# Projections of a hybrid attention layer on 16-bit parts instead of 32-bit parts

## The chip, the cores and the metric

The kernel runs on one core of a Trainium2 chip. A core has a matrix engine (TensorE, in the profile PE, with its weight loads as PEld), three engines for elementwise work (VectorE = DVE, ScalarE = ACT, GpSimd = POOL), a queue that issues transfers (SyncE = SP) and 16 DMA engines. Each engine works through its own instructions in the order in which they stand; semaphores make one engine wait for another. The metric is the device time of one launch in microseconds, lower is better.

## The reference

One layer over a sequence of 1024 positions with width 1024. The input is normalised and modulated, then one input projection gives everything that 16 heads of 64 need; 8 heads are softmax attention with a forget gate, 8 are stick-breaking attention; each head's output is gated, and one output projection and a second normalisation follow.

```python
u = _layer_norm(x) * (1.0 + scale) + shift            # scale, shift, gate from silu(c) @ w_ada + b_ada
h = u @ w_in                                           # q, k, v, gate of each group, 8 forget logits
fox: s = q k^T / 8 + F_q - F_k ; causal ; softmax ; p v
sb:  z = q k^T / 8 ; w_ij = sigmoid(z_ij) * prod of sigmoid(-z_im) for j < m < i ; w v
y = concat(y_fox * silu(fg), y_sb * silu(sg)) @ w_out
out = _layer_norm(ALPHA * x + gate * y, ln_g, ln_b)    # all float32
```

## The kernel before, in words

**Precision.** Each large product is made of three matmuls on two parts of each operand: a first part of fewer bits and the rest. In the input projections both parts are of type f32r (`u_hi`, `u_lo` and, for the weights, `whi`, `wlo`; the profile's 32-bit matmuls, written f32). In the products of the attention weights with v, from pair 2 on, both sides are in 16-bit floats (f16).

**Work.** The heads are taken in 8 pairs. Pairs 0 to 3 are stick-breaking heads, 4 to 7 forget-gate heads. A pair has 16 units (head, row block of 128 queries): unit 0 to 15 of pair 0 are here called units 0 to 15, the next are 16 and on. Pair 0 takes row blocks 0 to 3 of both heads first, so that units 8 to 11 are row blocks 4 to 7 of its first head and 12 to 15 those of its second. A stick-breaking unit goes through these steps: scores `S` on PE (L611, L613); two sigmoids on ACT into `kp` (L646) and `be` (L648); a running product over `kp` on DVE (L654, L658); the product `be * kp` on POOL (L660). In pairs 0 and 1 PE then turns `be` (L691, tile `T`), ACT and DVE take it out of PSUM in two parts (L693, L694), and PE multiplies with v (L720). Two units lie between a unit's scores and its turn: the scores of unit k + 2 stand on PE behind the turn of unit k.

**Projections as filler.** The projection of pair 0 (and parts of pair 1) is made in a start phase. The others are generators that are cut into steps; a step of a q, k or gate projection is three matmuls of 512 columns (`m_step`, L329 to L331), a step of a v projection six of 256 or 264 (`v_tile`, L441 to L443). A table of numbers (`FILL`, by pair) sets how many steps stand between the units on PE. In `order` of names: tile `m_p_x_c` is the projection of pair p, x = 0 for q, 1 for k, 2 for gate, of half c of the sequence.

**Preparing weights.** `fetch_w` (L140 to L146) loads 512 columns of a weight matrix (256 KB), and POOL makes the two parts: a copy with rounding (L144) and a subtraction (L145). This happens for 50 pieces in the filler phase. For v of groups 1 to 3 a bound is needed, too, since what v meets there is in f16: `gen_ranges` loads those 12 pieces a second time and DVE sums their squares (L396), all in pair 0.

**What sets the order.** PE's order is the order of the program. On ACT, DVE and POOL a scheduler puts the instructions into an order before the run; on the chip this order is fixed.

**End.** The last gate projection (`gen_last_g`) runs in the first units of pair 7; between its steps the output weights are put in two parts (L1071 on ACT, L1072 on DVE and POOL), into the room of `u_hi` and `u_lo`. Then the output projection follows (L1112 to L1114).

## Time and profile before

Three runs: 665.35, 664.29 and 663.5 us, median 664.29 us. The profiled execution took 664.71 us; its span in the profile is 663.0 us, so 1.7 us lie around it. Times below are microseconds from the span's start.

| part | from, to | span | PE | DVE | ACT | POOL |
|---|---|---|---|---|---|---|
| start phase | 0 to 79.6 | 79.6 | 77.5 | 62.1 | 47.8 | 31.0 |
| pair 0 | 79.6 to 148.8 | 69.2 | 61.7 | 58.3 | 42.3 | 47.9 |
| pair 1 | 148.8 to 221.6 | 72.8 | 72.8 | 54.0 | 44.7 | 41.1 |
| pair 2 | 221.6 to 285.9 | 64.3 | 61.8 | 56.1 | 47.9 | 47.4 |
| pair 3 | 285.9 to 346.1 | 60.2 | 60.2 | 49.8 | 44.4 | 42.6 |
| pairs 4 to 6 | 346.1 to 523.6 | 177.5 | 177.1 | 133.0 | 123.8 | 65.9 |
| pair 7 | 523.6 to 585.0 | 61.4 | 54.1 | 46.8 | 41.4 | 38.0 |
| end | 585.0 to 663.0 | 78.0 | 70.4 | 51.7 | 5.5 | 30.4 |

The columns are busy time. A matmul counts as busy from its start to its modelled end, and the next one starts well before that end, so what a matmul costs in a row of matmuls is read from the distance between starts. POOL's columns and those of the other elementwise engines can be added up.

### The profile page before, as it was taken

To read this page: it belongs to the slowest core of one execution; us is meant where nothing else is said; L and a number is where in the kernel's file an instruction comes from. 1 tells how busy PE (TensorE), PEld (TensorE's weight loads), DVE (VectorE), ACT (ScalarE), POOL (GpSimd) and SP (SyncE) were. 2 spreads that over 40 slices of the span, in tenths; PEclk is the share of its full clock that TensorE was granted. 3 is DMA by queue.
4 is the path that set the end of the run, shared out by engine and by line. 5 is a ranking of instruction groups with operands and counts; after the bars stand their busy time and mean duration, and the time that the engine had idled before them with its cause. 6 is when DMAs were issued, how large, how long until landed. Compare 5 with 4: busy or idle time off the path is not lost. (4 is left out here: it accounts for less than half of the span.)

```text
span 663.0 us, 10902 instructions
## 1 busy us (share of the span) xinstructions
PE 635.6 (96%) x3558; PEld 535.5 (81%) x3558; DVE 511.8 (77%) x1011; ACT 397.8 (60%) x833; POOL 344.3 (52%) x429
## 2 busy tenths in 40 slices
PE   8999989799999999999999999999999979999995
PEld 5789878688899877788998888889888857788884
DVE  6787889886867797978877685867678875986656
ACT  5577347575656867767867675767668886530000
POOL 5660177666645677778666333330643266475412
PEclk9999989899999999999999999999999989999998
DMA  9983543321210255858476666666496997983201
GB/s 319 402 312 135 167 123 110 104 58 28 58 33 10 71 115 112 160 118 157 106 172 153 174 139 153 139 147 125 115 198 137 245 284 176 205 232 129 94 33 63
DMA packets 153800, 96.25 MB, mean 145 GB/s; under 512 B 118224, under 2 KB 133136, under 8 KB 153744
## 3 DMA queue, kind: packets, MB, share of 16 engines
q1 hardware_dynamic: 152160, 91.09, 54.1%
q10 hardware_dynamic: 1584, 4.47, 2.2%
q8 instruction: 28, 0.46, 0.3%
q14 instruction: 28, 0.23, 0.1%
HBM read 55.13 MB, written 7.90 MB: 95 GB/s over the span
## 5 line engine op out<-in xcount | busy, mean ns | idle before, releaser
L329 PE MATMUL m<-uh,whi 128*128 128x512 f32 x304 | 123.0, 405 | 1.2 <-DVE kl L316 1.2
L331 PE MATMUL m<-uh,wlo 128*128 128x512 f32 x304 | 119.8, 394 | 0.0
L330 PE MATMUL m<-ul,whi 128*128 128x512 f32 x304 | 119.8, 394 | 0.0
L660 POOL TENSOR_TENSOR be<-be,kp 128x127 f32<-128x127 f32 (+3 forms) x64 | 89.9, 1405 | 44.9 <-DVE kp L658 24.2
L741 POOL TENSOR_TENSOR ty<-ty,sg 64x256 f32<-64x256 f32 x64 | 49.8, 779 | 91.6 <-DVE ty L736 56.0
L654 DVE TENSOR_TENSOR_SCAN kp<-kp,floor 128x128 f32<-128x128 f32 (+3 forms) x64 | 58.5, 914 | 14.8 <-ACT kp L646 14.1
L611 PE MATMUL S<-k,q 128*128 128x512 f32 (+4 forms) x192 | 68.5, 358 | 1.0 <-ACT be L648 1.0
L331 PEld LDWEIGHTS m<-uh,wlo 128*128 128x128 f32 x304 | 57.2, 188 | 13.6
L329 PEld LDWEIGHTS m<-uh,whi 128*128 128x128 f32 x304 | 57.4, 189 | 12.0 <-PE m L331 1.2
L613 PE MATMUL S<-kl,qz 128*128 128x512 f32 (+4 forms) x192 | 65.8, 344 | 0.0
L330 PEld LDWEIGHTS m<-ul,whi 128*128 128x128 f32 x304 | 57.4, 189 | 9.7
L622 DVE CUSTOM_DVE_ANT_0 a<-S,fb 128x1024 f32<-128x1024 f32 (+7 forms) x64 | 48.2, 753 | 19.7 <-PE S L613 15.8
L628 ACT ACTIVATE a<-a,nm 128x1024 f32<-128x1024 f32 (+7 forms) x64 | 49.7, 776 | 19.8 <-DVE nm L622 18.9
L638 DVE SCALAR_TENSOR_TENSOR home<-a,l,home 128x1024 f16<-128x1024 f32 (+7 forms) x64 | 58.1, 907 | 3.5 <-ACT home L634 3.3
L634 ACT ACTIVATE home<-a,l 128x1024 f16<-128x1024 f32 (+7 forms) x64 | 49.3, 773 | 16.2 <-DVE l L630 9.0
L646 ACT ACTIVATE kp<-S 128x384 f32<-128x384 f32 (+4 forms) x96 | 43.7, 491 | 23.7 <-PE S L613 21.9
L709 PE MATMUL pv<-home,v_g 128*128 128x256 f16 x480 | 56.3, 265 | 0.7 <-DVE ty L736 0.7
L709 PEld LDWEIGHTS <-v_g 128*128 128x128 f16 x480 | 44.2, 99 | 15.1 <-issue 9.8
L441 PE MATMUL v<-whi_v,uh 128*128 128x256 f32 (+1 forms) x192 | 54.7, 285 | 0.0
L443 PE MATMUL v<-wlo_v,uh 128*128 128x256 f32 (+1 forms) x192 | 54.4, 283 | 0.0
L442 PE MATMUL v<-whi_v,ul 128*128 128x256 f32 (+1 forms) x192 | 54.1, 282 | 0.0
L1112 PE MATMUL o<-woh,whi_y 128*128 128x512 f32 (+1 forms) x119 | 47.4, 398 | 5.4 <-DVE sg L322 4.8
(327 smaller groups left out, 1614.3 us busy)
## 6 DMA issues: line engine op xcount, KB each, us to landing
raw<-in_w_qkg_dram SPq DMA_DIRECT2D x38, 256.0 KB, 2.8
wss<-in_w_ss_dram SPq DMA_DIRECT2D x14, 512.0 KB, 8.4
x<-in_x_dram SPq DMA_DIRECT2D x8, 512.0 KB, 6.9
...
```

The source lines that it names most:

```text
L329: nc.tensor.matmul(acc, hi[:, c], u_hi[kt][:, s], start=(kt == 0), stop=False)
L330: nc.tensor.matmul(acc, hi[:, c], u_lo[kt][:, s], start=False, stop=False)
L331: nc.tensor.matmul(acc, lo[:, c], u_hi[kt][:, s], start=False, stop=(kt == NB - 1))
L441: nc.tensor.matmul(acc[:, :n], u_hi[kt][:, ts_], hi[:, s], start=(kt == 0), stop=False)
L442: nc.tensor.matmul(acc[:, :n], u_lo[kt][:, ts_], hi[:, s], start=False, stop=False)
L443: nc.tensor.matmul(acc[:, :n], u_hi[kt][:, ts_], lo[:, s], start=False, stop=(kt == NB - 1))
L611: nc.tensor.matmul(S[:, s, :w], qst[p][h][:, qs], kst[p][h][:, ks], start=True, stop=False)
L613: nc.tensor.matmul(S[:, s, :w], z, klo[p][:, ks], start=False, stop=not masked)
L638: lows[:] = [nc.vector.scalar_tensor_tensor(lo, ab, l, hi, op0=ALU.mult, op1=ALU.subtract)]
L654: last_dve = nc.vector.tensor_tensor_scan(rv, rv, floor[:, :ke - lo], initial=0.0, op0=ALU.mult, op1=ALU.max)
L660: nc.gpsimd.tensor_tensor(be[:, :ke - 1], be[:, :ke - 1], kp[:, 1:ke], op=ALU.mult)
L709: nc.tensor.matmul(acc[:, q0:256], vt[p][:, kb, h * P:(h + 1) * P], pt[:, 2 * kb + x_, q0:], start=(kb == 0 and x_ == 0), stop=(kb == last ...
```

## The change

From the gate projection of pair 1 on, u and the weights are used as two f16 parts each, still with three matmuls per product. To keep f16 in range, u is scaled with a bound (the largest |scale| + |shift|), and each weight matrix with its norm. The norms of one to three matrices ("a batch", 13 in all) are made together: ACT squares and sums the raw pieces (`square`), PE sums over partitions, DVE and POOL make the factors (`scales`); the inverse factors are folded into the instructions that take the results out of PSUM. u is converted once, in 16 pieces of 128 x 512 (`u_convert`): POOL adds `u_hi` and `u_lo` into one room `u_sum`, ACT makes the first part, DVE the rest; the results take the room of `u_hi`. One room serves all 16 pieces, so POOL's next sum waits until ACT and DVE have read the one before. `split16` puts a weight piece in parts: for pairs up to 3 ACT makes the first part, and POOL scales and subtracts; for later pairs POOL does all three. `gen_ranges` and its second loads are gone. Pair 1's gate and pair 2's q and k are taken half by half, with tiles of v between them, and the steps in which nothing was done are taken out of `FILL`. The output weights take other rooms.

```diff
+    C0 = (4, 3.2)
+    C1 = (34, 3.4)
+    BATCHES = (
+        ((14, 1), 22, 26, (((1, 2), (28, 29)), ((2, 0), (33, 37)))),
+        ((30, 1), 35, 38, (((2, 1), (41, 44)),)),
+        ((36, 2), 46, 50, (((1, 3), (52, 54, 56, 58)),)),
...
     def m_step(acc, tiles, kt, ch):
-        hi, lo = tiles[kt // 4]
+        two = tiles[kt // 4]
         c = slice((kt % 4) * P, (kt % 4) * P + P)
-        s = slice(ch * 512, ch * 512 + 512)
-        nc.tensor.matmul(acc, hi[:, c], u_hi[kt][:, s], start=(kt == 0), stop=False)
-        nc.tensor.matmul(acc, hi[:, c], u_lo[kt][:, s], start=False, stop=False)
-        nc.tensor.matmul(acc, lo[:, c], u_hi[kt][:, s], start=False, stop=(kt == NB - 1))
+        nc.tensor.matmul(acc, two[:, 0, c], u_part(kt, 0, ch), start=(kt == 0), stop=False)
+        nc.tensor.matmul(acc, two[:, 0, c], u_part(kt, 1, ch), start=False, stop=False)
+        nc.tensor.matmul(acc, two[:, 1, c], u_part(kt, 0, ch), start=False, stop=(kt == NB - 1))
...
+    def u_convert(kb, ch):
+        if not u_rooms:
+            u_rooms.append(raw_tile("u_sum"))
...
+        full = u_rooms[0]
+        nc.gpsimd.tensor_tensor(full, u_hi[kb][ch].bitcast(F32), u_lo[kb][ch].bitcast(F32), op=ALU.add)
+        nc.scalar.activation(two[:, 0, :], full, AF.Copy, scale=u_up)
+        nc.vector.scalar_tensor_tensor(two[:, 1, :], full, u_up, two[:, 0, :], op0=ALU.mult, op1=ALU.subtract)
...
-        for g in range(1, 4):
-            n = 528 if g == 1 else 512
-            for h in range(4):
-                raw = raw_tile(f"n{g}_{h}")[:, :n]
-                nc.sync.dma_start(raw, w_vf[h] if g == 1 else w_v[g - 1, h])
-                at = 4 * g - 4 + h
-                nc.vector.tensor_tensor_reduce(out=raw, in0=raw, in1=raw, op0=ALU.mult, op1=ALU.add, scale=1.0,
-                                               scalar=0.0, accum_out=fr[:, at:at + 1])
...
+    def square(batch):
+        at = 6 * (n_batch[0] % 2)
+        for i, key in enumerate(k for pm in batch for k in halves_of(*pm)):
+            raw = raw16[key]
+            nc.scalar.activation(rooms[1].bitcast(BF16)[:, :raw.shape[1]], raw, AF.Square,
+                                 accum_out=sums[:, at + i:at + i + 1])
...
+    def scales(batch, ps_n):
...
+        nc.vector.tensor_copy(sums16, sums[:, at:at + n])
+        nc.tensor.matmul(ps_n[:, :n], ones16.to_broadcast([P, P]), sums16, start=True, stop=True)
...
+            nc.vector.tensor_reduce(out=n2[:, x_:x_ + 1], in_=ps_n[:, col:col + k], op=ALU.add,
+                                    axis=mybir.AxisListType.X)
...
+        nc.gpsimd.tensor_tensor(up, n2[:, :k], mhalf.to_broadcast([P, k]), op=ALU.pow)
+        nc.gpsimd.tensor_scalar(up, up, 28800.0, None, op0=ALU.mult)
...
+            nc.vector.tensor_scalar(at, w_up[p, m], u_up, UNIT[m], op0=ALU.mult, op1=ALU.mult)
+            nc.vector.reciprocal(at, at)
...
+    def split16(key, home=None):
...
+        if p < 4 and (p, m) != (3, 3):
+            nc.scalar.activation(hi, raw, AF.Copy, scale=w_up[p, m])
+            nc.gpsimd.tensor_scalar(raw, raw, w_up[p, m], None, op0=ALU.mult)
+        else:
+            nc.gpsimd.tensor_scalar(raw, raw, w_up[p, m], None, op0=ALU.mult)
+            nc.gpsimd.tensor_scalar(hi, raw, 1.0, 1.0, op0=ALU.mult, op1=ALU.mult)
+        nc.gpsimd.tensor_tensor(lo, raw, hi, op=ALU.subtract)
...
-    FILL = (52, 72, 68, 68, 72, 72, 58, 16)
+    for kb in range(NB):
+        at_step(C0[0] + int(C0[1] * kb), u_convert, kb, 0)
+        at_step(C1[0] + int(C1[1] * kb), u_convert, kb, 1)
...
+    FILL = (52, 64, 60, 62, 64, 66, 50, 16)
```

All 16 pieces of u are converted within pair 0. At three places the order of the instructions is shown. The first is POOL in pair 0 from the product of unit 8 (`be_0_0_4`: pair 0, head 0, row block 4) to that of unit 9 (`be_0_0_5`), before:

```order
L660 TENSOR_TENSOR be_0_0_4_1236<-be_0_0_4_1236,kp_0_0_4_1235 128x639
L145 TENSOR_TENSOR wlo_2_0_1_1560<-raw_2_0_1_1557,whi_2_0_1_1559 128x512
L741 TENSOR_TENSOR ty_0_1_0_1244<-ty_0_1_0_1244,sg_0_548 64x256
L661 MEMSET be_0_0_5_1295 128x1
L660 TENSOR_TENSOR be_0_0_5_1295<-be_0_0_5_1295,kp_0_0_5_1294 128x767
```

and with the change, where L793 is the old L660, L876 the old L741, L1103 the gate bias work that stood at units 2 and 3 before, L541 the subtraction of `split16`, and L372 the sum of `u_convert` (its number of the piece and the half stand behind `uh`):

```order
L793 TENSOR_TENSOR be_0_0_4_1307<-be_0_0_4_1307,kp_0_0_4_1306 128x639
L876 TENSOR_TENSOR ty_0_1_0_1315<-ty_0_1_0_1315,sg_0_565 64x256
L541 TENSOR_TENSOR w_2_0_0_1338<-raw_2_0_0_1035,w_2_0_0_1338 128x512
L541 TENSOR_TENSOR w_2_0_1_1406<-room_0_941,w_2_0_1_1406 128x512
L1103 TENSOR_TENSOR wlo_gate_0_1343<-gate_91,whi_gate_0_1342 128x512
L372 TENSOR_TENSOR u_sum_936<-uh_7_0_141,ul_7_0_157 128x512
L1103 TENSOR_TENSOR wlo_gate_1_1347<-gate_91,whi_gate_1_1346 128x512
L372 TENSOR_TENSOR u_sum_936<-uh_0_1_128,ul_0_1_144 128x512
L372 TENSOR_TENSOR u_sum_936<-uh_1_1_130,ul_1_1_146 128x512
L794 MEMSET be_0_0_5_1380 128x1
L793 TENSOR_TENSOR be_0_0_5_1380<-be_0_0_5_1380,kp_0_0_5_1379 128x767
```

Seven instructions on whole pieces stand between the two products now, where there were two. The second place is ACT between the sigmoids of the same two units, with the change (L779 and L781 are the old L646 and L648, L473 the squares, L373 the first part of a piece of u, L826 the old L693):

```order
L781 ACTIVATE be_0_0_4_1307<-S_0_0_4_1301 128x640
...
L373 ACTIVATE u16_6_0_1134<-u_sum_936,wsc_96 128x512
L473 ACTIVATE room_1_959,modc_159<-raw_1_3_0_1397 128x528
L373 ACTIVATE u16_7_0_1181<-u_sum_936,wsc_96 128x512
L473 ACTIVATE room_1_959,modc_159<-raw_1_3_1_1463 128x528
L373 ACTIVATE u16_0_1_1363<-u_sum_936,wsc_96 128x512
L473 ACTIVATE room_1_959,modc_159<-raw_1_3_2_1475 128x528
L826 CAST pt_0_1_1_0_1291<-T_0_1_3_0_1367 128x4x128
L779 ACTIVATE kp_0_0_5_1379<-S_0_0_5_1374 128x384 x2
```

The sigmoid of unit 9 stands behind three conversions of u, each of which waits for POOL's sum. The third place is POOL at the end of pair 0, from the product of unit 15 (`be_0_1_7`) on, with the change; `w_1_3` are the four pieces of v for pairs 2 and 3 with the forget logits, and L537 is the scaling of `split16`:

```order
L793 TENSOR_TENSOR be_0_1_7_1719<-be_0_1_7_1719,kp_0_1_7_1718 128x1023
L537 TENSOR_SCALAR raw_1_3_0_1397<-raw_1_3_0_1397,bss_sb_102 128x528
L537 TENSOR_SCALAR raw_1_3_1_1463<-raw_1_3_1_1463,bss_sb_102 128x528
L537 TENSOR_SCALAR raw_1_3_2_1475<-raw_1_3_2_1475,bss_sb_102 128x528
L537 TENSOR_SCALAR raw_1_3_3_1520<-raw_1_3_3_1520,bss_sb_102 128x528
L794 MEMSET be_1_0_0_1778 128x1
L793 TENSOR_TENSOR be_1_0_0_1778<-be_1_0_0_1778,kp_1_0_0_1777 128x127
L541 TENSOR_TENSOR w_1_3_0_1731<-raw_1_3_0_1397,w_1_3_0_1731 128x528
L876 TENSOR_TENSOR ty_0_1_2_1784<-ty_0_1_2_1784,sg_0_565 64x256
L541 TENSOR_TENSOR w_1_3_1_1745<-raw_1_3_1_1463,w_1_3_1_1745 128x528
```

PE needs both of these weight pieces there (L579 to L581 are the old L441 to L443) before it turns unit 15 (L824, the old L691) and makes the scores of unit 17 (L744):

```order
L579 MATMUL v_1_0_1812<-w_1_3_1_1745,u16_2_0_980 128x264
...
L581 MATMUL v_1_0_1812<-w_1_3_1_1745,u16_3_0_1009 128x264
L824 MATMUL T_0_1_7_0_1829<-ident_69,be_0_1_7_1719 128x128 x4
L824 MATMUL T_0_1_7_1_1836<-ident_69,be_0_1_7_1719 128x128 x4
L744 MATMUL S_1_0_1_1843<-k_1_0_282,q_1_0_280 128x256
```

Before, PE's filler at this place was the q projection of pair 2, whose weights POOL had made ready earlier in pair 0; now it is the first tile of v of pairs 2 and 3, whose weights follow the product of unit 15 on POOL.

More of the change, by code (lines that the diff above doesn't have):

```diff
@@ L146, in fetch_w @@
         return hi, lo
-    def fetch_half(p, m, h):
-        return fetch_w(f"{p}_{m}_{h}", w_qkg[p, m, h], 512)
-    def fetch_m(p, m):
-        return [fetch_half(p, m, h) for h in range(2)]
+    wsc = cp.tile([P, 32], F32, tag="wsc", name="wsc")
     E = mybir.EngineType
@@ L375, in tile_hybrid_layer, with gen_range @@
     v_evacs = []
-    v_up, v_down, v_two = {}, {}, {}
-    def gen_ranges():
-        for _ in range(NORM_AT):
-            yield
+    v_two = {}
+    def gen_range():
         nc.gpsimd.tensor_copy(modc[:, 1, :], bss_sb[:, 1, :])
+        nc.gpsimd.memset(ones16, 1.0)
         m2 = rng[:, 0:2]
@@ L400, in gen_ranges @@
-        row = t_tile("u_row")[0:1, :P]
-        nc.tensor.transpose(row, rng[:, 2:3], ident)
-        nc.vector.tensor_reduce(out=rng[0:1, 3:4], in_=row, op=ALU.max, axis=mybir.AxisListType.X)
-        yield
-        yield
-        yield
-        yield
-        ps_r = t_tile("ranges")
-        nc.tensor.matmul(ps_r[:, 0:1], ones[0:1, :].to_broadcast([1, P]), rng[0:1, 3:4], start=True, stop=True)
-        nc.tensor.matmul(ps_r[:, 4:16], ones.to_broadcast([P, P]), fr, start=True, stop=True)
+        yield
@@ L410, in gen_ranges @@
+        row = pv_tile("u_row")
+        nc.tensor.transpose(row[0:1, :P], rng[:, 2:3], ident)
+        nc.vector.tensor_reduce(out=rng[0:1, 3:4], in_=row[0:1, :P], op=ALU.max, axis=mybir.AxisListType.X)
+        for _ in range(U_WAIT):
+            yield
+        nc.tensor.matmul(row[:, P:P + 1], ones[0:1, :].to_broadcast([1, P]), rng[0:1, 3:4], start=True, stop=True)
         top = rng[:, 4:5]
-        nc.vector.tensor_scalar(top, ps_r[:, 0:1], 1.0e-30, None, op0=ALU.max)
+        nc.vector.tensor_scalar(top, row[:, P:P + 1], 1.0e-30, None, op0=ALU.max)
@@ L420, in gen_ranges, with at_step, load_raw @@
-        nc.vector.tensor_scalar(down, down, 1.0 / UP, None, op0=ALU.mult)
-        for g in range(1, 4):
-            v_up[g], v_down[g] = up[:, g - 1:g], down[:, g - 1:g]
+        nc.vector.tensor_scalar(u_up, top, 900.0, None, op0=ALU.mult)
+    prep = {}
+    def at_step(n, make, *args):
+        prep.setdefault(n, []).append((make, args))
+    raw16, n_raw = {}, [0]
+    rooms = []
+    def load_raw(key):
+        p, m, h = key
+        src, n = (w_qkg[p, m, h], 512) if m < 3 else (w_vf[h], 528) if p == 1 else (w_v[p - 1, h], 512)
+        n_raw[0] += 1
+        if n_raw[0] % 6 == 4 and n == 512:
+            t = rooms[0]
+        else:
+            t = sb.tile([P, 528], F32, tag="wlo", bufs=RING, name=f"raw_{p}_{m}_{h}")
+        raw16[key] = t[:, :n]
+        nc.sync.dma_start(raw16[key], src)
@@ new lines, in halves_of @@
+    def halves_of(p, m):
+        return [(p, m, h) for h in range(2 if m < 3 else 4)]
+    n_batch = [0]
+    def square(batch):
[4 more added lines that the diff above has]
+                                 accum_out=sums[:, at + i:at + i + 1])
+    UNIT = {0: 1.0 / SCALE, 1: 1.0, 2: 2.0, 3: 1.0}
+    asked = []
@@ new lines, in tile_hybrid_layer @@
+    n_inv, w_up = [0], {}
+    def split16(key, home=None):
+        p, m, h = key
+        raw = raw16.pop(key)
+        n = raw.shape[1]
+        if home is None:
+            two = sb.tile([P, 2, 528], F16, tag="whi", bufs=RING, name=f"w_{p}_{m}_{h}")
+        else:
+            two = sb.tile([P, 2, 512], F16, tag=f"v{home}", bufs=1, name=f"w_{p}_{m}_{h}")
+        w16.setdefault((p, m), []).append(two)
+        hi, lo = two[:, 0, :n], two[:, 1, :n]
+        if p < 4 and (p, m) != (3, 3):
+            nc.scalar.activation(hi, raw, AF.Copy, scale=w_up[p, m])
+            nc.gpsimd.tensor_scalar(raw, raw, w_up[p, m], None, op0=ALU.mult)
+        else:
+            nc.gpsimd.tensor_scalar(raw, raw, w_up[p, m], None, op0=ALU.mult)
+            nc.gpsimd.tensor_scalar(hi, raw, 1.0, 1.0, op0=ALU.mult, op1=ALU.mult)
+        nc.gpsimd.tensor_tensor(lo, raw, hi, op=ALU.subtract)
@@ L424, in tile_hybrid_layer, with gen_prep @@
+    def gen_prep():
+        n = 0
+        while prep:
+            for make, args in prep.pop(n, ()):
+                if make is split16 and args[0][:2] not in w_up:
+                    at_step(n + 1, make, *args)
+                else:
+                    make(*args)
+            n += 1
+            yield
     rng = bss_sb.rearrange("p k i -> p (k i)")
+    sums = modc.rearrange("p k i -> p (k i)")
+    ones16 = rng[:, 15:16].bitcast(BF16)[:, :1]
+    u_up = wsc[:, 28:29]
     def make_v(g):
@@ L822, in start_steps @@
                 for n in ns:
-                    nc.tensor.matmul(accs[n], w[n][i], u_hi[kb][:, s], start=(first and i == 0), stop=False)
+                    nc.tensor.matmul(accs[n], w[n][i], u_hi[kb][a // 512], start=(first and i == 0), stop=False)
         if 1 in parts:
             for n in ns:
-                nc.tensor.matmul(accs[n], w[n][0], u_lo[kb][:, s], start=False, stop=last)
+                nc.tensor.matmul(accs[n], w[n][0], u_lo[kb][a // 512], start=False, stop=last)
     for t in range(2, 4):
@@ L1059, in tile_hybrid_layer @@
     raw_wo = {}
+    WO_AT = [[(f"v{pr + x_}0", f"v{pr + x_}1") for x_ in (0, 4)] for pr in range(4)] + [
+        [(f"u{pr}0", f"u{pr}1"), (f"u{q}0", f"u{q}1")] for pr, q in ((7, 0), (1, 2), (3, 4), (5, 6))]
     def load_wo(pr):
```

214 lines of the change are left out of this document (138 added, 76 removed), and 10 rows, old and new, of the table BATCHES.

## Prediction, on record before the changed kernel ran

> **What bounds the kernel now.** I read the page's busy shares first, then a table of busy time by stretch cut at the pair boundaries (the first scores of each pair), then single rows. The columns of the table are span, PE, PEld, DVE, ACT, POOL busy with their counts, granted TensorE clock, DMA share and GB/s.
>
> ```profile
> PE 635.6 (96%) x3558; PEld 535.5 (81%) x3558; DVE 511.8 (77%) x1011; ACT 397.8 (60%) x833; POOL 344.3 (52%) x429
> 79.60:148.80 69.20, 61.71 (x337) 53.12 (x336) 58.25 (x101) 42.32 (x101) 47.87 (x59) 0.93 0.35 94
> 148.80:221.60 72.80, 72.80 (x462) 65.48 (x461) 53.95 (x106) 44.72 (x104) 41.07 (x58) 1.00 0.15 37
> 221.60:285.90 64.30, 61.81 (x320) 49.89 (x319) 56.10 (x66) 47.91 (x100) 47.44 (x56) 1.00 0.56 119
> 285.90:346.10 60.20, 60.20 (x404) 54.01 (x403) 49.83 (x72) 44.39 (x95) 42.64 (x53) 1.00 0.64 138
> 523.60:585.00 61.40, 54.07 (x279) 44.64 (x278) 46.78 (x112) 41.37 (x91) 37.96 (x38) 0.94 0.91 227
> ```
>
> In pairs 1 and 3 PE is busy for the whole stretch, at full clock: there a cheaper matmul shortens the run. Pair 0 is another stage: PE leaves 7.5 of 69.2 us free, at a clock of 0.93, and waits for the chain of the attention units. That chain runs through POOL, as these rows of POOL and PE show (start, duration, and in brackets the idle time before and what ended it):
>
> ```profile
> 115.49 1.30 POOL L145 TENSOR_TENSOR wlo<-raw,whi 128x512 fp32r<-128x512 f32 x1
> 116.87 1.08 POOL L741 TENSOR_TENSOR ty<-ty,sg 64x256 f32<-64x256 f32 x1
> 118.36 1.54 POOL L660 TENSOR_TENSOR be<-be,kp 128x767 f32<-128x767 f32 x1 [0.25 <-DVE kp L658]
> 123.54 2.27 POOL L660 TENSOR_TENSOR be<-be,kp 128x895 f32<-128x895 f32 x1 [3.52 <-DVE kp L658]
> 149.59 2.00 POOL L660 TENSOR_TENSOR be<-be,kp 128x1023 f32<-128x1023 f32 x1 [1.84 <-DVE kp L658]
> ```
> ```profile
> 115.59 0.66 PE L691 MATMUL T<-ident,be 128*128 128x128 f32 x4 [0.90 <-POOL be L660]
> 119.95 0.87 PE L691 MATMUL T<-ident,be 128*128 128x128 f32 x6
> 152.74 0.36 PE L611 MATMUL S<-k,q 128*128 128x256 f32 x1
> ```
>
> PE turns a unit as soon as POOL has its product (unit 9's ends at 119.9, its turn starts at 119.95), and the scores two units later stand behind that turn. Unit 15's product ends at 151.6; the scores of unit 17 start at 152.74. So a delay of POOL in pair 0 passes to PE. In the rest of the program PE is the bound, so a delay there isn't won back by idle time.
>
> **The gain: cheaper matmuls.** What a matmul costs in a row of matmuls is the distance between starts.
>
> ```profile
> 301.01 0.40 PE L329 MATMUL m<-uh,whi 128*128 128x512 f32 x1
> 303.57 0.39 PE L331 MATMUL m<-uh,wlo 128*128 128x512 f32 x1
> 195.04 0.28 PE L441 MATMUL v<-whi_v,uh 128*128 128x264 f32 x1
> 197.47 0.28 PE L443 MATMUL v<-wlo_v,uh 128*128 128x264 f32 x1
> 341.00 0.28 PE L442 MATMUL v<-whi_v,ul 128*128 128x256 f32 x1
> 342.91 0.28 PE L443 MATMUL v<-wlo_v,uh 128*128 128x256 f32 x1
> ```
> ```profile
> 575.81 1.20 PE pv L709 x12
> 598.99 1.66 PE pv L709 x16
> ```
> ```profile
> L329 PE MATMUL m<-uh,whi 128*128 128x512 f32 x304 | 123.0, 405 | 1.2 <-DVE kl L316 1.2
> L329 PEld LDWEIGHTS m<-uh,whi 128*128 128x128 f32 x304 | 57.4, 189 | 12.0 <-PE m L331 1.2 <-issue 0.8 <-DVE sg L322 0.4
> L709 PEld LDWEIGHTS <-v_g 128*128 128x128 f16 x480 | 44.2, 99 | 15.1 <-issue 9.8 <-DMA wor<-in_w_out_dram 0.3
> ```
>
> Eleven distances in 2.56 us make 0.2327 us for a 32-bit matmul of 512 columns; 20 in 2.43 make 0.1215 for 264 columns; 16 in 1.91 make 0.1194 for 256. For f16 this program has only the products with v: in the chain of waits 12 of them (ten of 256 columns, two of 128) take 1.20 us and 16 (fourteen and two) 1.66, which is 0.109 and 0.111 per 256 columns, say 0.110. No f16 matmul of 512 columns is in the trace; two of 256 make 0.220, which I take, with nothing saved (0.2327) and 0.2180 as its ends. The weight load becomes shorter (99 for 189 ns), but at 189 it already fits into 0.2327, so that is worth nothing. 304 steps of three make 912 matmuls of 512 columns, and v has 384 of 256 and 192 of 264: 912 x 0.0127 = 11.6, 384 x 0.0094 = 3.6, 192 x (0.1215 − 0.1134) = 1.6, together **16.8 us**, 18.7 with the lower end for 512 columns (912 x 0.0147 = 13.4).
>
> For a warm row of matmuls the Trainium skill ("TensorE: Matmul & The Clock Gate", on the gap between consecutive issues) gives the columns over 2.4 GHz and some 2.5 ns more, 215.7 ns at 512; by it the 32-bit row of 232.7 ns is 17 ns over that floor, and the whole gain would be an estimated 21 us instead of 16.8.
>
> Not all of the 16.8 arrives. The part in pair 0, 19 of the 304 steps or 57 x 0.0127 = 0.7, shortens nothing, since PE waits there. In pairs 2 and 3 DVE is busy for 56.1 of 64.3 and 49.8 of 60.2 us, and ACT gets squares and first parts; PE already lost 2.5 us in pair 2, and I take off 3 (ends 0 and 6, the latter twice what is lost now). Pair 7 gets something back:
>
> ```profile
> 541.64 0.47 PE L1112 MATMUL o<-woh,whi_y 128*128 128x512 f32 x1 [3.61 <-DVE sg L322]
> ```
>
> Here PE waits 3.61 us for the last gate, whose evacuation stands behind the conversions of the output weights on ACT; in the change fewer of these stand ahead of it. I take 1.5 (ends 0 and 3.6). So **14.6 us** arrive.
>
> **The price: POOL in pair 0.** Each kind of instruction has its nearest row; the last row is the window from the first product of pair 0 to the end of its last.
>
> ```profile
> L145 POOL TENSOR_TENSOR wlo<-raw,whi 128x512 fp32r<-128x512 f32 x38 | 50.1, 1322 | 2.0
> L144 POOL TENSOR_SCALAR whi<-raw 128x512 fp32r<-128x512 f32 x38 | 25.8, 680 | 26.3 <-PE m L330 12.1 <-PE v L442 6.2 <-DMA raw<-in_w_qkg_dram 4.3
> L417 POOL TENSOR_TENSOR bss_sb<-bss_sb,mhalf 128x3 f32<-128x3 f32 x1 | 0.9, 878 | 0.0
> L660 POOL TENSOR_TENSOR be<-be,kp 128x127 f32<-128x127 f32 (+7 forms) x15 | 20.4, 1362 | 10.9 <-DVE kp L658 5.6 <-DVE kp L654 5.3
> 80.80:151.60 70.80, 63.31 (x345) 54.47 (x344) 60.09 (x104) 43.20 (x103) 49.78 (x61) 0.93 0.34 93
> ```
>
> Added to POOL ahead of unit 15's product: 16 sums of u at 1.30 (a subtraction of the same shape is 1.30 in the row at 115.49) = 20.8; three batches of factors at 0.88 and some 0.22 = 3.3; six scalings of pieces (L537) at 0.68 = 4.1; six subtractions (L541) at 1.30 = 7.8; one scaling of the gate, 0.7. That is 36.7. Removed: seven pieces in two parts (six of pairs 1 and 2, one of v) at 1.32 + 0.68 = 14.0. Net **+22.7**. POOL was busy for 49.8 of 70.8 us and idle for 21.0, so even without any idle time it now needs 72.5 us: unit 15's product ends no earlier than 80.8 + 72.5 = 153.3, 1.7 later than now.
>
> Behind that product POOL's order has four scalings of v pieces (2.7), the product of unit 16 (0.4 by its size), one subtraction (1.3), one gate product (0.7) and a second subtraction (1.3), 6.4 us, and PE needs both pieces before unit 15's turn; then come some six v matmuls (0.7) and the turn. Before, the turn came 0.35 after the product. So the scores of unit 17 are late by at least 1.7 + 6.4 + 0.7 − 0.35 = **8.4 us**.
>
> How much idle time stays is the unknown. Of the 21.0 us, 10.9 were waits of the product for DVE's running product. This chain (sigmoids on ACT, scan on DVE, product on POOL, turn on PE) doesn't get shorter, and it now waits in queues with more in them: between the products of units 8 and 9 POOL has seven whole pieces and a gate product, some 9.8 us, where it had 2.4, and the units after gain nothing from that time, since the scores of unit 11 stand behind unit 9's turn. So I keep the 10.9. To this come the waits for the one room: where sums stand side by side on POOL, the second waits for ACT's and DVE's readings.
>
> ```profile
> L809 ACT CAST hw<-raws 128x512 fp32r<-128x512 f32 x5 | 3.1, 621 | 4.1 <-DMA raws<-in_w_qkg_dram 4.1
> 121.73 0.67 DVE L396 CUSTOM_DVE_ANT_0 n<-n 128x512 f32<-128x512 f32 x1
> 124.67 1.69 DVE L396 CUSTOM_DVE_ANT_0 n<-n 128x512 f32<-128x512 f32 x1
> ```
>
> The first part takes ACT 0.62 and the rest DVE some 0.75 (between the two rows of L396, near the lower), so such a wait is 1.4. There are three such places; I take two (2.7). Delay: 8.4 + 10.9 + 2.7 = **22 us**. Lower end 8.4 (all idle time filled). Upper end 30: 8.4 + 10.9 + 4.2 for three places, and at each of them the sigmoid behind the conversions on ACT waits for a sum and a conversion more, 3 x 1.9 = 5.8.
>
> What else pair 0 gets is covered by that: ACT takes 16 first parts, and squares and first parts of weights, some 20 us on 42 busy of 69; DVE loses the norms (10.8 us) and gets 16 rests (12) and the factors. In a run PE idles more, so the clock in pair 0 will fall below 0.93, as it did with the waits of now; PE isn't the bound there, and I give that no price.
>
> **Sum.** 664.7 (the profiled execution) + 22.0 − 14.6 = 672.1; this execution was 0.4 above the median, so **671.7**.
>
> **The rivals.**
>
> *POOL packs.* If POOL works ahead in what were its waits, the delay stays between 8.4 and 12.6 (the 8.4 and 40% of the 10.9), and the time is 664.3 + 8.4 − 14.6 = 658.1 to 662.3: **faster**. For it: the sums wait for nothing but their room, so a wait for the scan may be spent before rather than after; against it: the order on POOL is fixed, and a product that isn't ready blocks the sums behind it. The place is POOL between units 8 and 15; it decides at a delay of 14.6, that is when less than 6.2 us of idle time stay there. With the larger gain (18.7) and nothing lost in pairs 2 and 3 it ends at 655.
>
> *It cancels.* A delay of 12.6 to 16.6 gives 662.3 to 666.3, within 0.3% (2 us, about what a measurement of this kernel can tell from no change).
>
> *DVE is held up by POOL.* The row at 124.67 took 1.69 us where its like at 121.73 took 0.67; it lay beside POOL's product from 123.54 to 125.81 and ended some 0.5 after it. The 16 new DVE instructions also read two operands while POOL is busy nearly throughout. Held up by 1.0 each they add up to 16 on DVE, and half of that on the chain gives 671.7 + 8 = 680, all of it 688. Against it: other instructions of DVE with two operands show their usual time beside POOL.
>
> The Trainium skill ("SBUF — State Buffer", on the engines' ports) says that a DVE instruction with two SBUF inputs and a GpSimd instruction that reads SBUF exclude each other for a whole instruction; the row at 124.67 agrees with it, and how often this meets the new instructions no run here shows.
>
> *The matmuls don't get cheaper.* If an f16 matmul of 512 columns starts every 0.2327 us and v's gain is 5.2 at most, the time is 664.3 + 22 − 3 = 683 or more. The products with v speak against it.
>
> **Chances.** Forecast (delay 16.6 to 30) 0.47; POOL packs 0.29; cancels 0.14; DVE held up 0.07; no cheaper matmuls 0.03. So faster 0.29, same 0.14, slower 0.57. The likeliest case's own range is 666 to 680. The range for all reaches down to 655, the end of the packing case, and up to 684, which takes in half of the case with DVE; some 0.1 is left out.
>
> **What would show it.** Right: projection matmuls of 512 columns starting every 0.22 us or less; POOL busy for over 65 us of pair 0's stretch; unit 9's product (767 columns) after 127; the scores of unit 17 at 169 to 182; from there on pairs shorter than now by 1 to 3 us each. Wrong: scores of unit 17 before 167 (packs); DVE's rests of u at over 1.3 us on average (held up); a pair from 1 on in which PE waits more than now, which would be a wait for parts made too late that I count at nothing, because each batch is asked for many units before its use; starts 0.23 apart.

## The result, and the profile after

The changed kernel takes 747.18 us (median of four runs, 746.53 to 749.39), the kernel before 663.89 in the same comparison: a ratio of 1.126, 95% interval 1.123 to 1.129. The forecast was 671.7 us, with a range from 655 to 684. The direction was right, the size wrong: 83 us more instead of 7.

The table of busy time by stretch of the changed kernel, cut at the first scores of each pair (span, PE, PEld, DVE, ACT, POOL busy with counts, granted TensorE clock, DMA share, GB/s):

```profile
81.10:176.80 95.70, 66.05 (x350) 48.87 (x349) 70.12 (x111) 63.26 (x146) 75.10 (x80) 0.88 0.17 49
176.80:261.70 84.90, 71.16 (x454) 51.16 (x452) 55.45 (x116) 56.62 (x133) 51.47 (x62) 0.94 0.14 38
261.70:336.80 75.10, 61.57 (x322) 34.35 (x319) 56.86 (x75) 52.66 (x112) 56.99 (x64) 0.94 0.48 99
336.80:410.20 73.40, 60.28 (x407) 41.72 (x404) 52.72 (x88) 52.59 (x114) 54.66 (x60) 0.97 0.58 112
605.20:745.20 140.00, 125.08 (x630) 100.89 (x628) 103.03 (x193) 45.60 (x97) 66.65 (x75) 0.95 0.57 153
```

Pair 0 takes 95.7 us where it took 69.2 and pair 1 84.9 for 72.8, but pairs 2 and 3 grew as well: 75.1 for 64.3 and 73.4 for 60.2. Pairs 4, 5 and 6 take 69.1, 67.2 and 58.7 for 61.5, 62.2 and 53.8. Only pair 7 with the end stays, 140.0 for 139.4. So 41.5 of the 83 us lie in pairs 2 to 6 and 38.6 in pairs 0 and 1. No stage behaves as forecast, in which pairs 1 to 6 were to get shorter.

The cheaper matmuls are there. PE's timeline of the changed kernel, first and last of nine in a row:

```profile
297.37 0.38 PE L355 MATMUL m<-u,w 128*128 128x512 f16 x1
...
299.09 0.38 PE L357 MATMUL m<-u,w 128*128 128x512 f16 x1
```

Eight distances in 1.72 us, 0.215 each, where the 32-bit ones stood 0.2327 apart. But PE is busy for 86% of the span where it was for 96%. The waits of PE in the changed kernel (what waits, for whom; us in total, times, longest) name what it stands for; the largest rows are:

```profile
PE gate L1112 <- POOL wlo_gate L1103: 13.8, 2, 12.6
PE v L581 <- POOL w L541: 13.6, 4, 9.6
PE m L357 <- POOL w L541: 13.6, 4, 4.0
PE pv L842 <- DVE ty L871: 6.5, 3, 3.7
PE T L824 <- POOL be L793: 6.2, 3, 4.4
PE m L355 <- DVE kl L333: 5.5, 2, 3.6
```

L541 is the last step of a weight piece's split: 27 us are waits for weights. Before, none of PE's waits of 0.5 us or more was for weights of a projection. And the groups of POOL show what a split costs (busy, mean ns of one):

```profile
L541 POOL TENSOR_TENSOR w<-raw,w 128x512 f16<-128x512 f32 (+1 forms) x43 | 50.0, 1178 | 0.2
L539 POOL TENSOR_SCALAR raw<-raw,bss_sb 128x512 f32<-128x512 f32 x23 | 36.7, 1608 | 0.6
L537 POOL TENSOR_SCALAR raw<-raw,bss_sb 128x512 f32<-128x512 f32 (+1 forms) x20 | 32.1, 1617 | 1.0 <-ACT w L536 0.8
L540 POOL TENSOR_SCALAR w<-raw 128x512 f16<-128x512 f32 x23 | 14.3, 634 | 0.9
```

Scaling a piece (L537, L539) takes 1.61 us, not the 0.68 of the conversion that was taken as its nearest row.

Three places show the kinds of stalls. **In pair 0** PE comes to the gate's terms, whose second part stands on POOL behind two subtractions of weights (first PE, then POOL):

```profile
127.38 0.80 PE L1112 MATMUL gate<-wlo_gate,half 128*128 128x512 f32 x1 [12.58 <-POOL wlo_gate L1103]
```
```profile
123.84 1.15 POOL L541 TENSOR_TENSOR w<-raw,w 128x512 f16<-128x512 f32 x1
124.95 1.15 POOL L541 TENSOR_TENSOR w<-room,w 128x512 f16<-128x512 f32 x1
126.06 1.26 POOL L1103 TENSOR_TENSOR wlo_gate<-gate,whi_gate 128x512 fp32r<-128x512 f32 x1
```

**At the end of pair 0** unit 15's product ends at 180.4 (the first row is that product). PE has stood since 178.8 at the first v tile, and waits for its weights, which follow that product on POOL:

```profile
178.44 2.00 POOL L793 TENSOR_TENSOR be<-be,kp 128x1023 f32<-128x1023 f32 x1 [2.04 <-DVE kp L791]
180.41 6.36 POOL L537 TENSOR_SCALAR raw<-raw,bss_sb 128x528 f32<-128x528 f32 x4
187.13 1.19 POOL L541 TENSOR_TENSOR w<-raw,w 128x528 f16<-128x528 f32 x1
```
```profile
188.37 0.38 PE L581 MATMUL v<-w,u 128*128 128x264 f16 x1 [9.60 <-POOL w L541]
192.83 0.56 PE L744 MATMUL S<-k,q 128*128 128x256 f32 x1
```

The scores of unit 17 start at 192.8, 40 us later than before. **In pair 2** stands a stall of the kind that pairs 3 to 5 have, too (waits for L540 or L541 in each), here that of the batch with q and k of pair 4. Its last two squares on ACT and the conversion of its sums on DVE, PE's matmul for the norms and the matmuls that wait, and POOL:

```profile
275.28 0.62 ACT L473 ACTIVATE room<-raw 128x512 bf16<-128x512 f32 x1
...
278.24 0.63 ACT L473 ACTIVATE room<-room 128x512 bf16<-128x512 f32 x1
...
280.44 0.45 DVE L492 CAST wsc<-modc 128x4 bf16<-128x4 f32 x1
```
```profile
309.86 0.17 PE L493 MATMUL pv<-wsc,bss_sb 128*128 128x4 bf16 x1
327.95 0.61 PE L355 MATMUL m<-u,w 128*128 128x512 f16 x1 [4.39 <-POOL be L794]
332.79 0.61 PE L357 MATMUL m<-u,w 128*128 128x512 f16 x1 [3.80 <-POOL w L541]
...
334.05 0.63 PE L357 MATMUL m<-u,w 128*128 128x512 f16 x1
```
```profile
315.31 0.72 POOL L504 TENSOR_TENSOR bss_sb<-bss_sb,mhalf 128x2 f32<-128x2 f32 x1
319.63 0.22 POOL L505 TENSOR_SCALAR bss_sb<-bss_sb 128x2 f32<-128x2 f32 x1
319.94 1.57 POOL L539 TENSOR_SCALAR raw<-raw,bss_sb 128x512 f32<-128x512 f32 x1
...
327.27 0.62 POOL L540 TENSOR_SCALAR w<-raw 128x512 f16<-128x512 f32 x1
...
331.58 3.38 POOL L541 TENSOR_TENSOR w<-raw,w 128x512 f16<-128x512 f32 x3
334.92 1.16 POOL L541 TENSOR_TENSOR w<-room,w 128x512 f16<-128x512 f32 x1
```

The pieces are squared by 278.9 and their sums converted by 280.9, but the matmul that sums the norms stands at 309.9 in PE's order, 31 us after the last square, and its row shows no wait in front of it. From it to the factors pass ten more (309.9 to 319.9, through queues of DVE and POOL), and then all four pieces are split at once, with all four subtractions last: 16 us (319.9 to 336.1). PE is ready for the first piece at 323.6 (327.95 less 4.39); its first part is done at 327.9, by the row of L540 (the row of PE names the small fill, L794, right behind it), and its second at about 332.7. The stall costs more than the wait: behind it the matmuls stand 0.42 us apart (three distances from 332.79 to 334.05), twice the 0.215 from above.

### The profile page after: what moved, and what is told of

Same layout as the page of the kernel before. It is cut to its first block, busy times and chain, and to the rows that moved or that the text cites. A ratio compares the mean times of both kernels' runs of the same rounds, so it can differ in the third digit from the quotient of the medians.

```text
span 745.2 us, 11146 instructions
## 1 busy us (share of the span) xinstructions
PE 638.0 (86%) x3569; PEld 446.9 (60%) x3569; DVE 540.5 (73%) x1099; ACT 455.1 (61%) x971; POOL 434.3 (58%) x500
## 5 line engine op out<-in xcount | busy, mean ns | idle before, releaser
L355 PE MATMUL m<-u,w 128*128 128x512 f16 x304 | 118.2, 389 | 17.8 <-DVE kl L333 5.5
L357 PE MATMUL m<-u,w 128*128 128x512 f16 x304 | 117.9, 388 | 13.6 <-POOL w L541 13.6
L356 PE MATMUL m<-u,w 128*128 128x512 f16 x304 | 117.3, 386 | 0.0
L793 POOL TENSOR_TENSOR be<-be,kp 128x127 f32<-128x127 f32 (+3 forms) x64 | 88.9, 1389 | 37.2 <-DVE kp L791 25.4
L876 POOL TENSOR_TENSOR ty<-ty,sg 64x256 f32<-64x256 f32 x64 | 53.9, 842 | 80.1 <-DVE ty L871 48.3
L744 PE MATMUL S<-k,q 128*128 128x512 f32 (+4 forms) x192 | 83.3, 435 | 5.0 <-ACT be L781 4.9
L581 PE MATMUL v<-w,u 128*128 128x256 f16 (+1 forms) x192 | 53.8, 280 | 16.9 <-POOL w L541 13.6
L746 PE MATMUL S<-kl,qz 128*128 128x512 f32 (+4 forms) x192 | 67.9, 355 | 0.0
L771 DVE SCALAR_TENSOR_TENSOR home<-a,l,home 128x1024 f16<-128x1024 f32 (+7 forms) x64 | 62.4, 975 | 2.8 <-ACT home L767 2.5
L842 PEld LDWEIGHTS <-v_g 128*128 128x128 f16 x480 | 48.1, 101 | 24.9 <-issue 12.9
L473 ACT ACTIVATE room<-raw 128x512 bf16<-128x512 f32 (+1 forms) x43 | 27.0, 628 | 58.6 <-DMA raw<-in_w_qkg_dram 28.2
L355 PEld LDWEIGHTS <-w 128*128 128x128 f16 x304 | 29.9, 98 | 54.8 <-issue 12.9
L357 PEld LDWEIGHTS <-w 128*128 128x128 f16 x304 | 30.1, 99 | 52.4 <-POOL w L541 16.0
L579 PE MATMUL v<-w,u 128*128 128x256 f16 (+1 forms) x192 | 54.3, 283 | 3.7 <-DVE v_g L589 1.6
L580 PE MATMUL v<-w,u 128*128 128x256 f16 (+1 forms) x192 | 53.8, 280 | 0.0
L779 ACT ACTIVATE kp<-S 128x384 f32<-128x384 f32 (+4 forms) x96 | 43.3, 486 | 14.7 <-PE S L746 12.6
```

What stands on the lines that cost most here:

```text
L355: nc.tensor.matmul(acc, two[:, 0, c], u_part(kt, 0, ch), start=(kt == 0), stop=False)
L356: nc.tensor.matmul(acc, two[:, 0, c], u_part(kt, 1, ch), start=False, stop=False)
L357: nc.tensor.matmul(acc, two[:, 1, c], u_part(kt, 0, ch), start=False, stop=(kt == NB - 1))
L579: nc.tensor.matmul(acc[:, :n], uh, hi[:, s], start=(kt == 0), stop=False)
L744: nc.tensor.matmul(S[:, s, :w], qst[p][h][:, qs], kst[p][h][:, ks], start=True, stop=False)
L746: nc.tensor.matmul(S[:, s, :w], z, klo[p][:, ks], start=False, stop=not masked)
```

## The experiments

Each kernel ran beside the kernel before on the same chip (661 to 667 us). Since the scheduler orders ACT, DVE and POOL anew for every edit, a run shows the edit together with its order. The last columns are stretches between first scores of pairs, from PE's timelines.

| run | time, us | pair 0 | pair 1 | pairs 2 to 6 |
|---|---|---|---|---|
| before | 663.9 | 69.2 | 72.8 | 302.0 |
| the change | 747.2 | 95.7 | 84.9 | 343.5 |
| nothing prepared | 637.5 | 58.9 | 67.6 | 289.9 |
| u only | 651.7 | 66.4 | 70.5 | 290.0 |
| weights only | 732.4 | 79.1 | 83.3 | 345.8 |
| scaling with two operations | 713.2 | 83.3 | 81.3 | 324.7 |
| no norms | 687.5 | 87.8 | 82.7 | 292.1 |
| no norms, scaling with two operations | 674.3 | 79.0 | 78.5 | 296.4 |
| rests on DVE | 701.5 | 78.5 | 80.9 | 319.8 |
| rests on DVE, gate parts off POOL | 695.5 | 73.1 | 80.9 | 319.2 |
| squares of a ready tile | 736.9 | 91.5 | 86.6 | 337.6 |
| splits with a constant | 717.3 | 88.8 | 85.8 | 319.6 |
| norms asked for earlier | 730.5 | 95.6 | 86.7 | 325.7 |
| fixed factors | 659.3 | 76.6 | 69.6 | 292.1 |
| fixed factors, gate parts off POOL | 664.0 | 79.1 | 70.5 | 291.3 |
| fixed factors, sums of u on DVE | 666.2 | 81.1 | 69.8 | 290.7 |

### What is prepared: nothing, u, the weights

```diff
     def load_raw(key):
+        return
     def square(batch):
+        return
     def ask_scales(batch):
+        for p, m in batch:
+            w_up[p, m] = inv[p, m] = one_cell
...
+        return
     def split16(key, home=None):
+        w16.setdefault((p, m), []).append(w_one[0])
+        return
     def u_convert(kb, ch):
+        u16[kb, ch] = u_rooms[0]
...
+        return
```

`one_cell` is a cell that holds 0.01; `w_one[0]` and `u_rooms[0]` are here tiles that are set once. All of this is in the first run; the second has only the edits of the weights, the third only that of `u_convert`. Where such a tile stands in, the products are of constants.

> All matmuls, evacuations and the rest as in the change, but nothing is prepared: the weight parts from the second pair's gate on are one constant tile, u's parts another, and the loads, squares, norms, splits and conversions are left out (so those products are of constants). The gain of the cheaper matmuls alone. If 912 matmuls of 512 columns start every 0.216 us and PE bounds the rest as before, 664 - 17 to 20 and a little more in pair 0, where POOL has less to do than before: 640 to 650 us. If the new order of the projections or the half-by-half filler costs by itself, it stays above 655.

> As the run without any preparation, but u is converted as in the change; the weight parts are one constant tile and their loads, squares, norms and splits are left out. Theory of the prediction (the price is POOL in pair 0, mostly the 16 sums): 15 to 22 us above the run without any preparation. Rival (the price is the weights' preparation, late in every pair): at most 10 above it.

> As the change, but u is not converted: its parts are one constant tile, the sums on POOL, first parts on ACT and rests on DVE are left out. Theory of the prediction: most of the loss goes, 665 to 690 us. Rival (weights' preparation): 710 to 735 us, with pairs 2 to 6 as long as in the change (75, 73, 69, 67, 59 us) and PE still waiting for POOL's subtraction (L541) in each.

Measured: 637.48 us (ratio 0.962, 0.956 to 0.967), 651.73 (0.983, 0.977 to 0.989), 732.38 (1.105, 1.097 to 1.113). So a gain exists, 25 us with nothing prepared, of which 12.1 lie in pairs 2 to 6 and the rest in pairs 0 and 1, which lose the preparation of the kernel before too. Converting u costs 14 us, between the two ranges that were expected (at most 10, or 15 to 22); but with u alone the scores of unit 17 start at 152.6, just as before the change: the sums fill the place of the split and the norms that are gone. The weights cost 95 us, and 56 of these in pairs 2 to 6 (345.8 for 289.9), where u costs nothing (290.0). The third run came out as its rival said: most of the price is the weights. In pair 0 the two don't simply add: u costs 7.5 us there by itself and 16.6 beside the weights (95.7 for 79.1), and the scores of unit 17 start at 175.2 with the weights alone and at 192.8 with both.

### The form of the scaling

```diff
-            nc.gpsimd.tensor_scalar(raw, raw, w_up[p, m], None, op0=ALU.mult)
+            nc.gpsimd.tensor_scalar(raw, raw, w_up[p, m], 1.0, op0=ALU.mult, op1=ALU.mult)
```

The edit stands in all three places where POOL scales (both branches of `split16`, and pair 1's gate).

> As the change in all results, but the scaling of a weight piece on POOL (L537, L539, L344) is written with two operations (times the factor, times 1.0) instead of one. In the change's trace one such scaling took 1.61 us where the conversion with two operations (L540) took 0.63. If the form with one operation is what costs, the 50 scalings take 0.65 us each, POOL loses 48 us of work and the time falls to 690 to 720; the scheduler's order also moves, since it prices the two forms differently. If the scalar read from memory is what costs, they stay at 1.6 us and the time at 735 to 760.

Measured: 713.21 us (1.076, 1.070 to 1.082). The groups of POOL in this run:

```profile
L539 POOL TENSOR_SCALAR raw<-raw,bss_sb 128x512 f32<-128x512 f32 x23 | 18.3, 810 | 0.7
L537 POOL TENSOR_SCALAR raw<-raw,bss_sb 128x512 f32<-128x512 f32 (+1 forms) x20 | 14.4, 730 | 1.2 <-ACT w L536 0.8
```

The same product with the factor from memory takes 0.73 and 0.81 us with a second operation behind it, 1.61 without: the form costs, not the factor. It brings 34 us, about half of it in pairs 0 and 1 (16.0), half in pairs 2 to 6 (18.8); the order that the scheduler makes from its price is in that number.

### Squares and norms

```diff
     def square(batch):
+        return
     def ask_scales(batch):
+        for p, m in batch:
+            w_up[p, m] = inv[p, m] = one_cell
...
+        return
```

> As the change, but the factors are one constant (0.01): the squares on ACT, PE's sums, and the steps that make the factors are left out; loads, scalings (still with one operation), first parts and subtractions stay. If the squares, which wait on ACT for loads (58 us of ACT's idle time in the change's trace ends with a load for a square) and hold up the sigmoids and read-outs behind them, are the second cause beside the scaling: 690 to 715 us. If the parts are late because of POOL's own work alone: 730 to 745 us.

> Both at once: constant factors without squares and norms, and the scaling with two operations. Beside the run with two operations alone (713 us) it shows what squares and norms cost when POOL's work is smaller. If the two causes add up: 665 to 690 us. If the squares only wait because POOL's scaling holds the rooms, taking them away changes little once the scaling is cheap: 700 to 713 us.

Measured: 687.50 us (1.033, 1.024 to 1.041) and 674.31 (1.013, 1.005 to 1.021). Pairs 2 to 6 in one row of the table of busy time, the change first, then the run without norms:

```profile
261.70:605.20 343.50, 297.14 (x1747) 184.48 (x1744) 249.45 (x561) 241.88 (x520) 210.04 (x225) 0.95 0.59 123
```
```profile
251.80:543.90 292.10, 282.55 (x1737) 179.58 (x1736) 240.84 (x499) 222.83 (x458) 186.87 (x201) 1.00 0.71 142
```

Without squares and norms these pairs take 292.1 us, 2 more than with nothing prepared, although POOL still scales with the dear form: there, what POOL does to the weights costs almost nothing once it may start when a piece has landed. By these rows PE is idle for 46.4 us in the change and for 9.6 without norms, which is 36.8 of the 51.4 us of difference; the other 14.6 are more busy time for nearly the same matmuls, with a granted clock of 0.95 instead of 1.00. In pairs 0 and 1 it is the other way round: leaving the norms out brings 10, and 44 remain over the run with nothing prepared. The two causes overlap: 60 and 34 us alone, 73 together, and with both gone 31 us remain in pairs 0 and 1 (157.5 for 126.5).

### Splits without POOL

In these two runs, and in the three with fixed factors further down, pair 1's gate is scaled with two operations as well.

```diff
-        if p < 4 and (p, m) != (3, 3):
-            nc.scalar.activation(hi, raw, AF.Copy, scale=w_up[p, m])
-            nc.gpsimd.tensor_scalar(raw, raw, w_up[p, m], None, op0=ALU.mult)
-        else:
...
-        nc.gpsimd.tensor_tensor(lo, raw, hi, op=ALU.subtract)
+        nc.scalar.activation(hi, raw, AF.Copy, scale=w_up[p, m])
+        nc.vector.scalar_tensor_tensor(lo, raw, w_up[p, m], hi, op0=ALU.mult, op1=ALU.subtract)
```

and, in the second run, also

```diff
-            nc.gpsimd.tensor_scalar(hi, gate[:, s], 1.0, 1.0, op0=ALU.mult, op1=ALU.mult)
-            nc.gpsimd.tensor_tensor(lo, gate[:, s], hi.bitcast(F32), op=ALU.subtract)
+            nc.scalar.copy(hi, gate[:, s])
+            nc.vector.tensor_tensor(lo, gate[:, s], hi.bitcast(F32), op=ALU.subtract)
```

> As the change in all results, but a weight piece goes in parts without POOL: ACT makes the first part of every piece, and DVE the rest in one instruction (raw times factor minus first part, as for u). POOL loses 115 us of work, ACT gets 28 more first parts (20 us), DVE 50 rests of some 0.75 us (38 us). If POOL in front of the products and the late parts is the cause, 655 to 690 us; if ACT's squares that wait for loads are, or DVE becomes the bound in pairs 2 and 3 (it was busy for 56 of 64 us there before), 690 to 725.

> As the run with the rests of the weights on DVE, and the two parts of the output gate's terms, which stand on POOL behind the split of weights and for which PE waited 13.8 us in pair 0 of the change, are made by ACT and DVE. If that wait is on the path by itself, 5 to 13 us less than the run beside it; if the products of the units end as late anyway, within 4 us of it.

Measured: 701.54 us (1.054, 1.047 to 1.061) and 695.52 (1.045, 1.037 to 1.052). With POOL out of the split, pairs 2 to 6 still take 319.8 us, 30 more than with nothing prepared: POOL's work isn't the whole cause there (DVE is busy for 270 us of them, 232 with nothing prepared, so it may be a part in its place). The gate's wait was worth 5.4 us in pair 0 here, of the 13.8 that the waits of PE show in the change.

### Which part of the norms

Three runs on the change itself. The squares read another tile:

```diff
+    wss_ready = gate
...
-            nc.scalar.activation(rooms[1].bitcast(BF16)[:, :raw.shape[1]], raw, AF.Square,
+            nc.scalar.activation(rooms[1].bitcast(BF16)[:, :raw.shape[1]], wss_ready[:, :raw.shape[1]], AF.Square,
```

> As the change, but ACT squares a tile that has long been ready (the output gate) in place of the weight pieces, so the same 50 squares are done and wait for no load; the factors then come from that tile's norm and not from the weights'. Without squares and norms pairs 2 to 6 took 61, 62, 58, 59 and 52 us, in the change 75, 73, 69, 67 and 59. If the squares' wait for loads is the cause: within 2 us each of the run without them, 690 to 700 us in all. If ACT's own work (50 x 0.82 us) or the chain of the factors is: 725 to 745.

The splits take a constant, in all three places of `split16` (one of them is shown):

```diff
-            nc.gpsimd.tensor_scalar(raw, raw, w_up[p, m], None, op0=ALU.mult)
+            nc.gpsimd.tensor_scalar(raw, raw, ones, None, op0=ALU.mult)
```

> As the change, with every square, norm and factor made as there, but the split of a weight piece uses a constant (1.0) in place of the factor, so it doesn't wait for the norm of its batch (the factors are still used where results are read out, so those don't fit). ACT, DVE and PE have the same work as in the change, and POOL too. Theory (the tie: a split may begin only when PE has come to the norms' matmul in its order, and then all pieces of a batch are due at once): pairs 2 to 6 fall from 75, 73, 69, 67, 59 to 61 to 64, 58 to 61, 53; 690 to 705 us. Rival (ACT's 41 us of squares hold up read-outs and sigmoids): pairs 2 to 6 stay above 70, 68, 65; 725 to 745.

The squares and norms stand right behind the loads, in ten batches (one of them is shown):

```diff
-        ((142, 2), 154, 158, (((4, 0), (168, 172)), ((4, 1), (182, 186)))),
+        ((142, 2), 149, 150, (((4, 0), (168, 172)), ((4, 1), (182, 186)))),
```

> As the change in all results; from the fourth batch on the squares and PE's norm matmul are asked for right behind the batch's last load, 2 to 8 of the filler's steps earlier. If the tie to PE's place is the cause, the parts come 2 to 6 us earlier per batch: 715 to 738 us. If PE then waits for squares whose loads wait for rooms, no better than 740.

Measured: 736.85 us (1.111, 1.109 to 1.114), 717.26 (1.081, 1.079 to 1.083) and 730.51 (1.101, 1.098 to 1.104). Pairs 2 to 6, squares of a ready tile first, then splits with a constant, then norms earlier:

```profile
259.20:596.80 337.60, 297.16 (x1747) 184.82 (x1745) 248.40 (x563) 238.00 (x507) 210.00 (x225) 0.96 0.60 125
```
```profile
255.70:575.30 319.60, 293.71 (x1747) 183.36 (x1745) 251.75 (x565) 240.16 (x514) 199.55 (x218) 0.97 0.64 131
```
```profile
263.40:589.10 325.70, 292.74 (x1747) 182.23 (x1745) 256.42 (x561) 238.87 (x517) 205.72 (x222) 0.98 0.62 129
```

The wait of the squares for loads, 58 us of ACT's idle time over the whole change, is worth only 6 of the 51 us that squares and norms cost there, so that explanation falls. The tie of the split to the norm is worth 24: with a constant, no wait for L541 is left among PE's, though all the work is done. Moving the norms a few steps brings 18 by the same lever. The other 27 were expected to go with the tie and did not: the time with a constant, 717 us, lies between the ranges of the theory and its rival. By its row they are 16 us more of idle PE than without squares and norms (25.9 for 9.6) and 11 more of busy time, at a granted clock of 0.97 for 1.00. In this run a split still waits for its piece's square, ACT is busy for 240 us where it is for 223 without squares, and PE's largest waits in these pairs are for the read-outs of q and k. It may be ACT's squaring in front of these read-outs, but no run shows that by itself; the cause of the 27 stays open.

### Fixed factors for the weights

```diff
     def square(batch):
+        return
     def ask_scales(batch):
+        for p, m in batch:
+            w_up[p, m] = 1.0
...
+            nc.vector.tensor_scalar(at, u_up, UNIT[m], None, op0=ALU.mult)
+            nc.vector.reciprocal(at, at)
...
     def split16(key, home=None):
-            nc.scalar.activation(hi, raw, AF.Copy, scale=w_up[p, m])
-            nc.gpsimd.tensor_scalar(raw, raw, w_up[p, m], None, op0=ALU.mult)
+            nc.scalar.activation(hi, raw, AF.Copy)
         else:
-            nc.gpsimd.tensor_scalar(raw, raw, w_up[p, m], None, op0=ALU.mult)
             nc.gpsimd.tensor_scalar(hi, raw, 1.0, 1.0, op0=ALU.mult, op1=ALU.mult)
```

The factor of v's read-out becomes 512 times larger in exchange. Two more kernels start from this one: one with the gate's parts on ACT and DVE as above, one with

```diff
-        nc.gpsimd.tensor_tensor(full, u_hi[kb][ch].bitcast(F32), u_lo[kb][ch].bitcast(F32), op=ALU.add)
+        nc.vector.tensor_tensor(full, u_hi[kb][ch].bitcast(F32), u_lo[kb][ch].bitcast(F32), op=ALU.add)
```

> All results are computed, with fixed factors for the weights in place of their norms: no squares, no norms, no scaling of weight pieces; a piece goes in parts as before the change (a conversion and a subtraction), u's bound stays. Each removed item showed as a cost on its own; without both, pairs 2 to 6 should take what they take without any preparation (60, 60, 58, 59, 52 us) and pairs 0 and 1 some 75 and 75: 650 to 668 us. If the conversion of u and the split together still hold POOL in pairs 0 and 1, 668 to 680.

> As the run with fixed factors, and the output gate's two parts are made by ACT and DVE, so that PE doesn't wait for them behind POOL's split in pair 0. That was worth 6 us where POOL had no split to do; here 3 to 8 us less than the run beside it, 645 to 662, faster than the kernel before by 0 to 15.

> As the run with fixed factors (659 us), and the sum of u's two parts is made by DVE instead of POOL: POOL loses 16 x 1.28 = 20.5 us in pair 0, DVE gets 16 x some 0.69 = 11 us. If POOL in front of the units' products is still the bound in pair 0 (76.6 us there, 58.9 with nothing prepared): 4 to 10 us less, 649 to 655. If DVE takes its place (58 of 69 us busy before), 657 to 664.

Measured: 659.27 us, a ratio of 0.994 (0.992 to 0.996). That is 88 us below the change and only 0.6% below the kernel before; its four runs (658.0 to 659.6) lie below all thirteen of that kernel (662.0 to 664.9). What it gives up is the fit of the factors to the weights: whether much larger or smaller weights would still fit 16 bits no run here shows. The other two are not faster, 664.04 (1.001, 1.000 to 1.002) and 666.15 (1.004, 1.002 to 1.005), and both lie above all that was expected of them. Pair 0 and pairs 2 to 6 of the first:

```profile
81.20:157.80 76.60, 64.12 (x346) 46.70 (x345) 65.67 (x136) 57.83 (x129) 65.59 (x72) 0.91 0.31 88
...
227.40:519.50 292.10, 283.75 (x1737) 179.85 (x1736) 234.71 (x498) 222.63 (x458) 141.14 (x167) 0.99 0.69 140
```

Pairs 2 to 6 are 9.9 us shorter than before, pair 0 is 7.4 longer, with DVE at 65.7 and POOL at 65.6 of 76.6 us. It fits this that moving work from POOL to DVE (and, for the gate, ACT) brought nothing, with pair 0 at 79.1 and 81.1 us; which wait held these runs was not followed further.

## Why the prediction was wrong

**The gain was right in kind and somewhat small.** "Two of 256 make 0.220, which I take" is 0.215 in the trace, so the 512-column matmuls save 912 x 0.0177 = 16.1 us and not 11.6; the Trainium skill's figure ("TensorE: Matmul & The Clock Gate", 215.7 ns at 512 columns) is what the trace shows. In the change no stage became shorter by it; with nothing prepared, pairs 2 to 6 are 12.1 us shorter than before.

**The step that failed** stands in the last paragraph of the prediction: a "wait for parts made too late that I count at nothing, because each batch is asked for many units before its use". What is asked early is the squares. The factor comes from a matmul at its place in PE's order, and only then may the splits begin: in pair 2, 31 us between the last square and that matmul, ten to the factors, 16 for the splits of the batch. Squares and norms together cost 51 us in pairs 2 to 6; the tie of the split to that matmul is 24 of them, and what the other 27 wait for stays open. The sum had this only as a part of the 3 us taken off in pairs 2 and 3, with 6 as its end. The clock, which the prediction expected to fall in pair 0 and gave no price, fell in pairs 2 to 6 as well (0.95 for 1.00), where PE is the bound.

**The second mis-sized term** was "six scalings of pieces (L537) at 0.68". The row taken was a conversion with two operations that writes rounded values (fp32r); the scaling writes f32 with one operation and takes 1.61. The bound from both sides was missing there: the subtraction of the same shape, 1.32 in a quoted row, was as near. The cheaper form brought 34 us over the whole program, its new order included. At the end of pair 0 the four scalings took 6.36 us for the 2.7 of the prediction, and the scores of unit 17 came 12.4 us after unit 15's product, where the prediction's terms give 7.9.

**Pair 0.** The place and the direction were right: POOL is busy for 75.1 us, and unit 9's product, expected after 127, starts at 138.1. The delay at unit 17's scores was forecast at 22 us, at most 30, and is 40. But the share of the parts was wrong: the 16 sums of u, the largest term, are no loss by themselves against the kernel before (152.6 for 152.7 at unit 17), while the weights alone delay unit 17 by 22 us; the sums cost another 18 only beside them (175.2 to 192.8). The order that I quoted also had the gate's second part behind two splits; I counted these instructions as POOL time and did not ask who on PE waits for them (12.6 us; taking the gate's parts off POOL brought 5.4 in pair 0, where POOL had no splits to do).

**The rivals.** None of them named the weights, and the time lies far above all their ranges. "DVE is held up by POOL" was right about the rests of u at most in a small way: they take 0.92 us on average for 0.75 assumed, below the 1.3 named as its sign. "The matmuls don't get cheaper" is out, with starts 0.215 apart. "POOL packs", with its 0.29, did not happen: POOL is idle for 20.6 us of pair 0 in the change (95.7 less 75.1), as it was before (21.3). Pair 7's 1.5 us did not arrive: 140.0 us with the end for 139.4.
